# Two-layer trunk on one core: all adaLN sums on TensorE, in four column groups of 32, by half chunks

## The chip, the cores and the metric

The kernel runs as one program on one of the eight NeuronCores of a Trainium2 chip. The metric is device time in microseconds (us) of one execution; lower is better. The engines are TensorE (PE in the profile; its weight loads are the row PEld), VectorE (DVE), ScalarE (ACT), GpSimd (POOL) and the DMA queue that SyncE issues (SP, in the profile SPq). All five run their own instruction streams in order and wait for each other by semaphores.

## What is computed

Two groups of tokens, 512 latent and 128 context, go through two layers with the same weights. Each layer is an adaLN-modulated RMSNorm, an input projection, four mixers (three attentions and an mLSTM), a gated merge with an output projection, then a second modulated RMSNorm and a SwiGLU feed-forward. The change concerns one small part of it, the adaLN vectors:

```python
def _adaln(cvec, w, b):
    m = jnp.dot(jax.nn.silu(cvec), w) + b
    return jnp.split(m, 6, axis=-1)

def _modulate(xn, shift, scale):
    return xn * (1 + scale) + shift
...
    sh1, sc1, gt1, sh2, sc2, gt2 = _adaln(c_ctx, w_mod[l], b_mod[l])
    h = _modulate(_rmsnorm(xp, norm1_g[l]), sh1, sc1)
    ...
    xp = xp + gt1 * _merge(...)
    xp = xp + gt2 * _swiglu(_modulate(_rmsnorm(xp, norm2_g[l]), sh2, sc2), w_ffn_in[l], w_ffn_out[l])
```

Per layer, two vectors of 1024 (one of each token group, called v = 0 and v = 1) are multiplied with a 1024 x 6144 matrix `w_mod[l]`. The 6144 columns are shift, scale and gate of the first norm (w = 0) and of the second (w = 1), each 1024 wide. Everything is float32, and the matrix of one layer is 25 MB.

## The kernel before, in words

**The main stream.** Weights come from HBM as 128 x 1024 blocks (`wload`, L399). ScalarE makes a rounded float32r copy `hi` (L404), VectorE the rest `lo` (L405), and TensorE forms each product with three float32r matmuls, hi by hi, hi by lo and lo by hi (`mm3`, L416 to L418). There are two raw buffers and five of each of hi and lo. From the fifth feed-forward column block on, the feed-forward runs a seven-product scheme in `ff_pair` (matmuls on L1825 to L1827), in which VectorE combines PSUM results between the products (L1839, L1843, L1846) before a PSUM bank may be used again; the weight splits of that part are on L453 and L454. PSUM has eight banks: three of `acc`, two each of `S` and `T`, one of `O`.

**The adaLN columns** are cut into chunks of 512, twelve to a layer. A chunk has eight k-tiles of 128 rows.

- *Chunks 0 to 3 of layer 0* (shift and scale of the very first norm) are made in `start()`. For the first four k-tiles of a chunk (two in the last chunk) VectorE multiplies the tile by the silu column of v and adds it to an accumulator 128 x 512 (L490, L492). The other k-tiles go to TensorE as plain float32 matmuls with two columns of weights (L608). Two matmuls with `sel` add the rows of the accumulators into the same PSUM bank (L610). Then the two rows are copied (L611), turned into columns with four transposes (L614) and stored in `modr` (L615). After the second and the fourth chunk, `mod_cols` (L645 to L647) and the modulation (L625, L628, L629) make half of `hT`, the input of the first projection.
- *The other 20 chunks* are the background, a generator `adaln_all` that is advanced by the main stream. A load brings one k-tile of 256 KB (L512, four buffers `wm`). VectorE sums v = 0 into `msum0` (L490, L492), ScalarE multiplies for v = 1 (L485) and GpSimd adds (L488). At the end of a chunk, eight 128 x 128 transposes put the sums on the free axis (L501), and VectorE reduces them to columns (L502). Gates go on through a bias (L528), a transpose (L532) and DRAM.

**What sets the order.** The kernel is recorded in one order, and a scheduler places each engine's instructions by priority. `tick()` (L390) is called at each step of the main stream and adds `bg[0]` to a credit; each whole credit advances the background by one step. The rate is 0.14 in the mixers, 0.8 in the last four merges of a layer (M20 to M23), 0.1 in the `ff_pair` part and 0.3 in the feed-forward's output products. `bg_until` runs the generator until the chunks that a norm or a gate needs are there.

```python
BG_MIX, BG_FREE, BG_PAIR, BG_OUT = 0.14, 0.8, 0.1, 0.3
...
    def tick():
        bg[1] += bg[0]
        bg_steps(int(bg[1]))
        bg[1] -= int(bg[1])
```

Of the kernel before, what the change touches and what calls it, by code (L numbers as in the profile page):

```python
# [17 lines left out]
P = 128  # L18
# [69 lines left out]

BG_MIX, BG_FREE, BG_PAIR, BG_OUT = 0.14, 0.8, 0.1, 0.3
# [137 lines left out]
def trunk(ctx: ExitStack, tc: tile.TileContext, a: dict, depth: int):  # L227
# [130 lines left out]
    V.memset(sel, 0.0)  # L358
    V.memset(sel[:, 0:4:3], 1.0)
# [14 lines left out]
    with tc.high_priority(offset=8 * WPRI):  # L374
        SY.dma_start(csil.rearrange("p k v -> p (k v)"), a["cc"])
        S.activation(csil, csil, AF.Silu)
    hT = cp.tile([P, KT, 2, NTOK], F32R, name="hT")
# [91 lines left out]


    bg_after = {}

    def newest():
        return list(nc.cur_bb.bb.instructions)[-1]

    def behind(eng):
        if eng in bg_after:
            after(newest(), bg_after.pop(eng), "the norm and what follows it go before the background")

    def adaln_acc(accs, w, kk, tmp=None):  # L480

        for v in range(2):
            s = csil[:, kk, v:v + 1]
            if v and tmp is not None:
                S.activation(accs[v][:, :512] if kk == 0 else tmp, w, AF.Copy, scale=s)  # L485
                behind("S")
                if kk:
                    G.tensor_tensor(accs[v][:, :512], accs[v][:, :512], tmp, ALU.add)  # L488
            elif kk == 0:
                V.tensor_scalar(accs[v][:, :512], w, s, None, ALU.mult)  # L490
            else:
                V.scalar_tensor_tensor(accs[v][:, :512], w, s, accs[v][:, :512], ALU.mult, ALU.add)  # L492
            if v == 0 and tmp is not None:
                behind("V")

    def adaln_cols(dst, accs):

        for v in range(2):
            ps = (bT if v else bS)()
            for j in range(4):  # L500
                T.transpose(ps[:, j * P:(j + 1) * P], accs[v][:, P * j:P * j + P], ident)  # L501
            V.tensor_reduce(dst(v), ps.rearrange("p (j n) -> p j n", j=4), AX.X, ALU.add)  # L502

    have = set()

    def adaln_all(items):


        def load(x):
            if x < KT * len(items):  # L510
                (l, ch), k = items[x // KT], x % KT
                SY.dma_start(wm_tiles[x % 4], a["w_mod"][l, P * k:P * k + P, 512 * ch:512 * ch + 512])  # L512
                behind("load")

        load(0)
        load(1)
        for i, (l, ch) in enumerate(items):
# [6 lines left out]
            if (ch // 2) % 3 == 2:  # L524
                adaln_cols(lambda v: gcol[:, 4 * v:4 * v + 4], msum)
                w, h = ch // 6, ch % 2
                for v in range(2):
                    V.tensor_tensor(gcol[:, 4 * v:4 * v + 4], gcol[:, 4 * v:4 * v + 4], bgate[:, l, w, 4 * h:4 * h + 4],  # L528
                                    ALU.add)
# [19 lines left out]
    def start():  # L549
# [49 lines left out]
        for x, ch in enumerate(order):  # L599
# [9 lines left out]
            for v in range(2):  # L609
                T.matmul(ps[:2], sel[:, 2 * v:2 * v + 2], accs[v][:, :512], start=False, stop=(v == 1))  # L610
# [1456 lines left out]
```

## Time and profile before

| | |
|---|---|
| median of 3 runs | 2729.99 us (2727.19 to 2732.35) |
| the profiled execution | 2728.15 us |
| its span (first to last instruction) | 2726.4 us |
| PE busy | 2665.0 us, 98% |
| DVE, ACT, POOL busy | 78%, 53%, 27% |
| mean granted TensorE clock | 0.996 of full speed |
| HBM read | 252.73 MB |

How to read it: a matmul's busy time includes its way through the array, which overlaps the next one, so a row's mean duration (some 310 ns) is more than the step from one matmul to the next (0.11 us at 256 columns). What a matmul costs is read from the step between starts. The idle time of PE is the span minus its busy time. The chain of work is followed back from the last instruction, at each step to what released it.

### The profile page before, as it was taken

The page shows a single profiled execution, that of the slowest core. Times are in us where ns is not written, and L with a number is a line of the kernel's source. Part 1 is how long each engine was busy: PE and PEld are TensorE (multiplying, and loading weights), DVE is VectorE, ACT ScalarE, POOL GpSimd, SP SyncE. Part 2 cuts the span into 40 slices and gives each one's busy share as a digit, 9 for nine tenths or more (in the row PEclk, how much of TensorE's full clock was granted, in tenths as well). Part 3 has the DMA queues.
Part 4 walks back from the last instruction along what each step waited for, and adds up shares of the span by engine and source line. Part 5 has one row for each costly group of instructions (what it writes and reads, how often), then busy time and mean ns, then how long its engine had stood idle before and what let it go on. Part 6 is the DMA issues. An engine that isn't in the chain of part 4 may idle for free.

```text
span 2726.4 us, 51965 instructions
## 1 busy us (share of the span) xinstructions
PE 2665.0 (98%) x19514; PEld 2618.7 (96%) x19514; DVE 2125.9 (78%) x4780; ACT 1434.3 (53%) x3298; POOL 732.1 (27%) x650
## 2 busy tenths in 40 slices
PE   8999999999999999999999999999999999999998
PEld 5999999999999999999999999999999999999998
DVE  8776668889978778888777866778888767586957
ACT  6864446666644543444468743556666545333433
POOL 2000112112035326454330101112002342243433
PEclk9999999999999999999999999999999999999999
DMA  7323322112135333333232332212112342222222
GB/s 279 103 88 101 110 66 87 49 52 91 47 122 188 99 109 102 112 101 109 93 104 92 119 92 88 92 62 71 58 56 78 126 160 75 83 85 78 86 90 74
DMA packets 123580, 264.29 MB, mean 97 GB/s; under 512 B 14192, under 2 KB 40144, under 8 KB 123328
## 3 DMA queue, kind: packets, MB, share of 16 engines
q1 hardware_dynamic: 123328, 260.97, 29.7%
q8 instruction: 153, 2.51, 0.4%
q14 instruction: 99, 0.81, 0.1%
HBM read 252.73 MB, written 7.95 MB: 96 GB/s over the span
## 4 chain that ended last, share of the span: by engine, by line
PE 81%; DVE 10%; ACT 3%; issue 3%; DMA 2%; POOL 1%; DVEq 0%; SPq 0%; POOLq 0%; ACTq 0%
PE acc L416 18%; PE acc L417 18%; PE acc L418 18%; PE acc L1825 3%; PE acc L1826 3%; PE acc L1827 3%; PE O L1243 2%; PE T L1233 2%; DVE msum L492 1%; PE O L1826 1%; PE O L1825 1%; PE O L1827 1%; DVE wlo L405 1%; DMA wm<-w_mod 1%; PE S L1200 1%
## 5 line engine op out<-in xcount | busy, mean ns | idle before, releaser
L416 PE MATMUL acc<-hT,whi 128*128 128x256 f32 (+1 forms) x2240 | 698.0, 313 | 11.6 <-DVE hT L688 5.6
L417 PE MATMUL acc<-hT,whi 128*128 128x256 f32 (+1 forms) x2240 | 696.7, 311 | 2.3 <-DVE hT L629 1.3
L418 PE MATMUL acc<-hT,wlo 128*128 128x256 f32 (+1 forms) x2240 | 693.1, 310 | 0.0
L404 ACT CAST whi<-raw 128x512 fp32r<-128x512 f32 (+1 forms) x488 | 298.9, 620 | 371.8 <-PE acc L417 172.6
L405 DVE TENSOR_TENSOR wlo<-raw,whi 128x512 fp32r<-128x512 f32 (+1 forms) x488 | 373.2, 768 | 130.6 <-ACT whi L404 124.4
L416 PEld LDWEIGHTS acc<-hT,whi 128*128 128x128 f32 x2240 | 420.5, 188 | 17.0 <-DVE hT L688 6.5
L417 PEld LDWEIGHTS acc<-hT,whi 128*128 128x128 f32 x2240 | 422.3, 189 | 5.7 <-DVE hT L629 2.1
L418 PEld LDWEIGHTS acc<-hT,wlo 128*128 128x128 f32 x2240 | 421.9, 188 | 0.8
L488 POOL TENSOR_TENSOR msum<-msum,mtmp 128x512 f32<-128x512 f32 x140 | 206.7, 1476 | 227.4 <-ACT msum L485 133.1
L1623 POOL TENSOR_TENSOR m<-m,f 128x256 f32<-128x256 f32 x96 | 98.8, 1031 | 485.1 <-DVE f L1621 319.3
L1651 POOL TENSOR_TENSOR big<-big,t 128x256 f32<-128x256 f32 x150 | 127.9, 862 | 241.1 <-DVE t L1650 234.8
L748 ACT CAST pth<-T 128x512 fp32r<-128x512 f32 (+1 forms) x232 | 117.9, 520 | 112.2 <-PE T L1233 53.9
L485 ACT ACTIVATE mtmp<-wm,csil 128x512 f32<-128x512 f32 x140 | 101.4, 724 | 127.6 <-POOL msum L488 114.9
L749 DVE TENSOR_TENSOR ptl<-T,pth 128x512 fp32r<-128x512 f32 (+1 forms) x232 | 137.4, 603 | 34.3 <-ACT pth L748 33.8
L416 PE MATMUL acc<-big,whi 128*128 128x256 f32 (+1 forms) x512 | 159.6, 312 | 4.0 <-ACT f L1615 4.0
L453 ACT CAST whi<-of 128x512 fp32r<-128x512 f32 x144 | 88.7, 620 | 141.5 <-PE acc L418 49.8
L416 PE MATMUL acc<-whi,m 128*128 128x256 f32 x560 | 157.6, 283 | 5.0 <-DVE t L1650 5.0
L1650 DVE TENSOR_TENSOR t<-acc,P 128x256 f32<-128x256 f32 x200 | 82.9, 420 | 102.1 <-PE acc L418 75.1
L418 PE MATMUL acc<-big,wlo 128*128 128x256 f32 (+1 forms) x512 | 160.8, 314 | 0.0
L417 PE MATMUL acc<-big,whi 128*128 128x256 f32 (+1 forms) x512 | 159.2, 311 | 0.0
L417 PE MATMUL acc<-wlo,m 128*128 128x256 f32 x560 | 156.7, 281 | 0.0
L418 PE MATMUL acc<-whi,m 128*128 128x256 f32 x560 | 156.5, 280 | 0.0
(464 smaller groups left out, 7905.1 us busy)
## 6 DMA issues: line engine op xcount, KB each, us to landing
raw<-wflat SPq DMA_DIRECT2D x236, 512.0 KB
wm<-w_mod SPq DMA_DIRECT2D x160, 256.0 KB
raw<-wflat SPq DMA_DIRECT2D x120, 256.0 KB
q<-wflat SPq DMA_DIRECT2D x48, 256.0 KB
kv<-nbias SPq DMA_DIRECT2D x16, 576.0 KB
kv<-mdr SPq DMA_DIRECT2D x16, 320.0 KB
big<-x_sample SPq DMA_DIRECT2D x8, 512.0 KB
P<-gt_d SPq DMA_DIRECT2D x32, 128.0 KB
```

What stands on the lines that cost most here:

```text
L404: S.copy(hi[:, :n], raw[:, s0:s0 + n])
L405: V.tensor_tensor(lo[:, :n], raw[:, s0:s0 + n], hi[:, :n].bitcast(F32), ALU.subtract)
L416: T.matmul(ps, lhs(k, 0), rhs(k, 0), start=(k == 0), stop=False)
L417: T.matmul(ps, lhs(k, 0), rhs(k, 1), start=False, stop=False)
L418: T.matmul(ps, lhs(k, 1), rhs(k, 0), start=False, stop=(k == kn - 1))
L488: G.tensor_tensor(accs[v][:, :512], accs[v][:, :512], tmp, ALU.add)
L748: S.copy(hi[:, :n], ps[:, :n])
L749: V.tensor_tensor(lo[:, :n], ps[:, :n], hi[:, :n].bitcast(F32), ALU.subtract)
L1651: (V if n == 3 else G).tensor_tensor(xs[tt][:, 256 * n:256 * n + 256], xs[tt][:, 256 * n:256 * n + 256], t[:, :256], ALU.add)
L1825: T.matmul(ps, f(0), ops[name](k, 0), start=first and k == 0, stop=False, **more)
L1826: T.matmul(ps, f(0), ops[name](k, 1), start=False, stop=False, **more)
L1827: T.matmul(ps, f(1), ops[name](k, 0), start=False, stop=k == 3, **more)
```

## The change

All adaLN sums are matmuls. The two silu columns of a k-tile are padded with zeros to a weight block of 32 columns, `cw[:, k, :]`. The eight k-tiles of a sum are dealt to four column groups of the array: k-tile k writes PSUM partitions 32 (k % 4) to 32 (k % 4) + 31, so each group adds two k-tiles up. A second small matmul ("turn") takes the copied sums as weights (128 x 128) and `sel` as the moving operand of two columns: `sel` has ones at 32 g + v, so it adds the four groups and turns rows to columns at once. `adaln_sums` and `adaln_turn` are used by the first norm with 512 columns, where VectorE copies the sums, and by the background with 256 columns (half a chunk), where ScalarE copies them.

The background has three buffers of 512 KB (four k-tiles of 256 columns) in place of four of 256 KB, two loads to a half chunk; a load waits for the four matmuls that read its buffer. Its rate is 0.15 in the mixers and stays so through M20 to M23; the other rates are gone, and it is not advanced in the feed-forward. In the recorded order, 13 of the 20 chunks are done by the end of layer 0's output projection and the last by the second merge of layer 1's mLSTM branch (M31); before, four of the chunks were made in layer 0's feed-forward and about four in each layer's M20 to M23.

```diff
-BG_MIX, BG_FREE, BG_PAIR, BG_OUT = 0.14, 0.8, 0.1, 0.3
+BG_MIX = 0.15
...
-    wm_tiles = [cp.tile([P, 512], F32, name=f"wm{i}") for i in range(4)]
-    msum = [cp.tile([P, 512], F32, name=f"msum{v}") for v in range(2)]
-    mtmp = cp.tile([P, 512], F32, name="mtmp")
+    wm_tiles = [cp.tile([P, 1024], F32, name=f"wm{i}") for i in range(3)]
+    msum = cp.tile([P, 256], F32, name="msum")
+    cw = cp.tile([P, 8, 32], F32, name="cw")
...
+    def adaln_sums(ps, w, n):
+        for k in range(KT):
+            g = 32 * (k % 4)
+            T.matmul(ps[g:g + 32, :n], cw[:, k, :], w(k), start=(k < 4), stop=(k >= 4))
+
+    def adaln_turn(pc, sums, n):
+        for j in range(n):
+            T.matmul(pc[:, 2 * j:2 * j + 2], sums[:, P * j:P * j + P], sel[:, 0:2], start=True, stop=True)
...
-            for k in range(KT):
-                adaln_acc(msum, wm_tiles[(KT * i + k) % 4], k, mtmp)
-                load(KT * i + k + 2)
-                yield True
...
+        for i, (l, ch, hf) in enumerate(halves):
+            ps = bS()
+            adaln_sums(ps, lambda k: wm_tiles[(2 * i + k // 4) % 3][:, 256 * (k % 4):256 * (k % 4) + 256], 256)
+            S.copy(msum, ps[:, :256])
+            load(2 * i + 3)
+            load(2 * i + 4)
+            yield True
+            pc = bT()
+            adaln_turn(pc, msum, 2)
...
         for x, ch in enumerate(order):
-            accs = [ofs.take() for _ in range(2)]
+            sums = ofs.take()
             ps = acc()
...
+            adaln_sums(ps, lambda k: bufs[4 * x + k // 2][k % 2], 512)
+            V.tensor_copy(sums[:, :512], ps)
             pc = acc()
+            adaln_turn(pc, sums, 4)
...
-            if name == "M20":
-                bg[0] = BG_FREE
...
-                    bg[0] = BG_PAIR
...
-                bg[0] = BG_OUT
```

Three places show what moves; rows are in program order, and no time is in them.

TensorE in the first norm, second and third chunk (ch 2 and ch 1): before, four k-tiles of each went to TensorE, then the two sums of VectorE's accumulators (`of`).

```order
L608 MATMUL acc_164<-kv_3_211,csil 2x512 x2
L614 MATMUL acc_163<-ident,of_1_356 128x2 x4
L608 MATMUL acc_164<-kv_4_212,csil 2x512 x2
L610 MATMUL acc_164<-of_3_378,sel 2x512
L610 MATMUL acc_164<-of_4_379,sel 2x512
L614 MATMUL acc_162<-ident,of_3_378 128x2 x4
L608 MATMUL acc_163<-q_1_215,csil 2x512 x2
L608 MATMUL acc_163<-q_2_216,csil 2x512 x2
```

Now all eight k-tiles are there, 32 rows high, and a turn of four (L485) ends each chunk.

```order
L480 MATMUL acc_162<-kv_1_208,cw 32x512
L480 MATMUL acc_162<-kv_2_209,cw 32x512 x2
L480 MATMUL acc_162<-kv_3_210,cw 32x512 x2
L480 MATMUL acc_162<-kv_4_211,cw 32x512 x2
L485 MATMUL acc_160<-sel,of_2_370 128x2 x4
L480 MATMUL acc_161<-kv_5_212,cw 32x512 x2
L480 MATMUL acc_161<-kv_6_213,cw 32x512 x2
L480 MATMUL acc_161<-q_1_214,cw 32x512 x2
L480 MATMUL acc_161<-q_2_215,cw 32x512 x2
L485 MATMUL acc_162<-sel,of_3_407 128x2 x4
```

The chunk's matmuls on TensorE go from six to eight, with no accumulator of VectorE to wait for.

TensorE in the mixers of layer 0: the transposes that ended a background chunk before stand between the matmuls of a projection.

```order
L418 MATMUL acc_164<-whi_140,hT 128x256
L501 MATMUL S_166<-ident,msum_69 128x128 x4
L416 MATMUL acc_164<-whi_141,hT 128x256
L417 MATMUL acc_164<-wlo_146,hT 128x256
L418 MATMUL acc_164<-whi_141,hT 128x256
```

Now half a chunk's eight narrow matmuls stand there together (in other places in two or more pieces), and the turn of two follows.

```order
L419 MATMUL acc_160<-hT,whi_140 128x384
L480 MATMUL S_164<-wm_67,cw 32x256 x4
L480 MATMUL S_164<-wm_65,cw 32x256 x4
L420 MATMUL acc_160<-hT,whi_140 128x384
L421 MATMUL acc_160<-hT,wlo_145 128x384
L419 MATMUL acc_160<-hT,whi_140 128x384
L420 MATMUL acc_160<-hT,whi_140 128x384
L485 MATMUL T_166<-sel,msum 128x2
L1463 MATMUL S_163<-kv_24_2375,P_155 128x129
L485 MATMUL T_166<-sel,msum 128x2
```

The 320 narrow matmuls of the background stand in 66 such unbroken runs: 22 of eight, 13 of four, 8 of five or seven and 23 of one to three.

VectorE in layer 0's feed-forward, at one `ff_pair`: before, the sums of the background (L492) stand between the combinations L1839, L1843 and L1846 that free the PSUM banks.

```order
L454 TENSOR_TENSOR wlo_147<-of_32_10072,whi_142 128x512
L492 SCALAR_TENSOR_TENSOR msum_69<-wm_67,csil,msum_69 128x512
L1839 TENSOR_TENSOR f_153<-acc_163,f_153 128x320
L454 TENSOR_TENSOR wlo_143<-q_24_10068,whi_138 128x512
L492 SCALAR_TENSOR_TENSOR msum_69<-wm_68,csil,msum_69 128x512
L1843 TENSOR_TENSOR f_153<-acc_164,f_153 128x320
L492 SCALAR_TENSOR_TENSOR msum_69<-wm_65,csil,msum_69 128x512
L1846 TENSOR_TENSOR f_152<-O_169,f_153 128x320
```

Now only the weight splits (L457) stand between the same combinations (L1817, L1821, L1824).

```order
L457 TENSOR_TENSOR wlo_145<-of_28_10065,whi_140 128x512
L1817 TENSOR_TENSOR f_151<-acc_161,f_151 128x320
L457 TENSOR_TENSOR wlo_141<-q_24_10061,whi_136 128x512
L1821 TENSOR_TENSOR f_151<-acc_162,f_151 128x320
L457 TENSOR_TENSOR wlo_142<-raw_134,whi_137 128x512
L1824 TENSOR_TENSOR f_150<-O_167,f_151 128x320
```

Three sums of the background have left this piece of VectorE's queue.

## Rows read from the trace of the kernel before

**Rows 1.** The page, busy time, share of the span and instructions by engine:
```profile
PE 2665.0 (98%) x19514; PEld 2618.7 (96%) x19514; DVE 2125.9 (78%) x4780; ACT 1434.3 (53%) x3298; POOL 732.1 (27%) x650
```

**Rows 2.** The page, chain that ended last, shares by engine:
```profile
PE 81%; DVE 10%; ACT 3%; issue 3%; DMA 2%; POOL 1%; DVEq 0%; SPq 0%; POOLq 0%; ACTq 0%
```

**Rows 3.** Stretches: us; busy PE, PEld, DVE, ACT, POOL; PE clock, DMA share, GB/s:
```profile
0.00:38.00 38.00, 29.14 (x100) 11.34 (x101) 29.23 (x76) 20.27 (x54) 4.77 (x12) 1.00 0.98 361
409.00:424.00 15.00, 12.91 (x82) 12.65 (x81) 14.81 (x27) 9.90 (x20) 6.40 (x5) 0.89 0.35 110
860.00:930.00 70.00, 68.28 (x556) 67.19 (x555) 51.86 (x95) 34.21 (x80) 37.08 (x35) 1.00 0.43 147
930.00:1290.00 360.00, 347.35 (x2537) 344.00 (x2537) 302.10 (x455) 154.31 (x297) 168.40 (x129) 0.99 0.33 106
1189.00:1198.00 9.00, 5.14 (x21) 4.89 (x20) 9.00 (x12) 3.44 (x7) 4.45 (x3) 0.63 0.43 128
2181.00:2290.00 109.00, 107.35 (x832) 106.56 (x830) 74.43 (x133) 51.58 (x114) 46.20 (x44) 1.00 0.35 121
2290.00:2720.00 430.00, 424.68 (x3168) 423.21 (x3168) 316.97 (x522) 163.95 (x330) 155.89 (x137) 1.00 0.26 84
```

**Rows 4.** Timeline of VectorE in layer 0's feed-forward (start, us, engine, line, operation):
```profile
1189.30 0.48 DVE L1839 TENSOR_TENSOR f<-acc,f 128x320 f32<-128x320 f32 x1
1189.70 1.35 DVE L454 TENSOR_TENSOR wlo<-q,whi 128x512 fp32r<-128x512 f32 x1
1190.98 1.75 DVE L492 SCALAR_TENSOR_TENSOR msum<-wm,csil,msum 128x512 f32<-128x512 f32 x1
1192.65 0.48 DVE L1843 TENSOR_TENSOR f<-acc,f 128x320 f32<-128x320 f32 x1
```

**Rows 5.** Timeline of PE at the same place (idle before, releaser in brackets):
```profile
1193.18 0.64 PE L1825 MATMUL acc<-hT,whi 128*128 128x320 f32 x1 [3.86 <-DVE f L1843]
```

**Rows 6.** Groups by line and shape: count, busy us, mean ns, idle before:
```profile
L492 DVE SCALAR_TENSOR_TENSOR msum<-wm,csil,msum 128x512 f32<-128x512 f32 x140 | 136.7, 976 | 5.0 <-DMA wm<-w_mod 3.6 <-DVE wlo L405 0.3
L501 PE MATMUL T<-ident,msum 128*128 128x128 f32 x80 | 13.4, 274 | 0.0
L501 PE MATMUL S<-ident,msum 128*128 128x128 f32 x80 | 12.5, 272 | 0.0
L610 PE MATMUL acc<-of,sel 128*2 128x512 f32 x16 | 7.5, 592 | 0.0
```

**Rows 7.** Chain that ended last, pieces (start, us, engine, output, line, count):
```profile
27.78 3.52 PE acc L608 x8
42.59 0.18 DVE modr L615
443.24 1.01 PE acc L1162 x10
694.59 0.87 PE T L1233 x8
872.62 8.38 DMA wm<-w_mod
```

**Rows 8.** Timeline of PE in the first norm, narrow and full-width matmuls in turn:
```profile
35.00 2.74 PE L608 MATMUL acc<-big,csil 128*2 128x512 f32 x6
37.67 0.38 PE L416 MATMUL acc<-hT,whi 128*128 128x256 f32 x1
37.98 1.02 PE L608 MATMUL acc<-big,csil 128*2 128x512 f32 x2
```

**Rows 9.** Timeline of PE in layer 0's mixers, around a gate's transpose (8 columns):
```profile
283.14 0.27 PE L532 MATMUL T<-ident,gcol 128*8 128x128 f32 x1
283.17 0.36 PE L418 MATMUL acc<-whi,hT 128*128 128x256 f32 x1
283.37 0.28 PE L416 MATMUL acc<-whi,hT 128*128 128x256 f32 x1
283.49 0.28 PE L417 MATMUL acc<-wlo,hT 128*128 128x256 f32 x1
```

More of the change, by code (lines that the diff above doesn't have):

```diff
@@ L376, in trunk @@
         S.activation(csil, csil, AF.Silu)
+    with tc.high_priority(offset=8 * WPRI):
+        V.memset(cw, 0.0)
+        V.tensor_copy(cw[:, :, 0:2], csil)
     hT = cp.tile([P, KT, 2, NTOK], F32R, name="hT")
@@ L468, in mod_slice @@
         return modr[:, w, s, 4 * (ch % 2):4 * (ch % 2) + 4, :]
[L471 to L502, printed above, removed]
-    have = set()
+    have = set()
+    modulated = [None]
+    def adaln_sums(ps, w, n):
+        for k in range(KT):
+            g = 32 * (k % 4)
+            T.matmul(ps[g:g + 32, :n], cw[:, k, :], w(k), start=(k < 4), stop=(k >= 4))
@@ L506, in adaln_all @@
+    def adaln_turn(pc, sums, n):
+        for j in range(n):
+            T.matmul(pc[:, 2 * j:2 * j + 2], sums[:, P * j:P * j + P], sel[:, 0:2], start=True, stop=True)
     def adaln_all(items):
+        halves = [(l, ch, hf) for l, ch in items for hf in range(2)]
         def load(x):
[L510 to L513, printed above, removed]
@@ L515, in adaln_all @@
-        load(0)
-        load(1)
-        for i, (l, ch) in enumerate(items):
-            for k in range(KT):
-                adaln_acc(msum, wm_tiles[(KT * i + k) % 4], k, mtmp)
-                load(KT * i + k + 2)
-                yield True
-            yield True
-            yield True
[L524 to L529, printed above, removed]
-                yield True
+            if x < 2 * len(halves):
+                (l, ch, hf), q = halves[x // 2], x % 2
+                c0 = 512 * ch + 256 * hf
+                SY.dma_start(wm_tiles[x % 3].rearrange("p (k n) -> p k n", k=4),
+                             a["w_mod"][l, 512 * q:512 * q + 512, c0:c0 + 256].rearrange("(k p) n -> p k n", p=P))
@@ new lines, in adaln_all @@
+        for x in range(3):
+            load(x)
+            after(list(nc.cur_bb.bb.instructions)[-1], modulated[0], "the first norm goes before the background")
+        for i, (l, ch, hf) in enumerate(halves):
[7 more added lines that the diff above has]
+            adaln_turn(pc, msum, 2)
+            view = pc[:, 0:4].rearrange("p (j v) -> p j v", j=2)
+            if (ch // 2) % 3 != 2:
+                V.tensor_copy(mod_slice(ch)[:, 2 * hf:2 * hf + 2, :], view)
+                if hf:
+                    have.add((l, ch))
+                yield True
+                continue
+            w, h = ch // 6, ch % 2
+            for v in range(2):
+                V.tensor_tensor(gcol[:, 4 * v + 2 * hf:4 * v + 2 * hf + 2], view[:, :, v],
+                                bgate[:, l, w, 4 * h + 2 * hf:4 * h + 2 * hf + 2], ALU.add)
+            yield True
+            if hf:
```

29 lines of the change are left out of this document (5 added, 24 removed).

## The prediction, made before the changed kernel ran

> **What bounds the kernel now.** I read the page first. PE is busy for 2665.0 of 2726.4 us, so it is idle for 61.4 us [rows 1], and 81% of the chain that ended last is PE, 10% DVE [rows 2]. A busy PE need not be at its peak, but the steps between its matmuls are steady: 0.12 us at 256 columns [rows 9]. So TensorE is the bound nearly everywhere. Work taken off VectorE, ScalarE and GpSimd can return at most the idle time of PE and what a low clock adds behind it; work put on TensorE is paid in full unless it runs inside the array beside other work. That is the balance to be drawn.
>
> The stretches then say where PE is idle [rows 3]. The first 38 us hold 8.9 us. Layer 0's feed-forward (930 to 1290 us), through which the background runs, holds 12.65 us in 360; layer 1's (2290 to 2720 us), with no background, 5.32 in 430. The two stages M20 to M23, with the fast background, hold 1.72 and 1.65 us. The largest single wait shows how it comes: two combinations of one `ff_pair`, L1839 and L1843, stand 3.35 us apart on VectorE because a weight split and an accumulation L492 of 1.75 us lie between them [rows 4]; PE waits 3.86 us for L1843 [rows 5]. The stretch from 1189 to 1198 us then has a granted clock of 0.63, which is some 6.7 of 9 us at the lower of the two levels, 1.2 GHz; PE had been idle just before [rows 3].
>
> **The change, part by part.** The sum is made against the profiled execution, 2728.15 us; the median of the runs, 2729.99, is 1.8 us above it, so the two agree within 0.1%.
>
> *Removed from PE:* 160 transposes L501 [rows 6]. Eight transposes of this shape take 0.87 us on the chain [rows 7], 0.109 each: -17.4 us.
>
> *Added, the turns:* 40 half chunks with two matmuls. A float32 matmul that is no transpose leaves two records: the code has eight calls of L610, the trace 16 records [rows 6]. So 160 records of two columns, with 128 columns of weights. L1162 is of that form, ten in 1.01 us [rows 7]: +16.2 us. Turns and transposes cancel.
>
> *Added, the sums:* 320 calls, 640 records of 256 columns. Eight records of 512 columns take 3.52 us [rows 7], and six are 2.74 us long with a duration of 0.592 for the last, so they start 0.43 us apart [rows 6, 8]; half the columns make 0.215. One after the other this is 640 x 0.215 = 137.6 us. No row shows matmuls in different column groups, since all narrow ones of before stand at the first columns, so I bound it from both sides. No overlap gives 137.6. If everything ran four abreast, 34.4. In between lies what the order of the records makes likely: the two records of a call go to the same group, one behind the other; if the engine starts its matmuls in order, the second record of a call can overlap only the first of the next call, which is in another group. Then each call costs one record, and an unbroken run costs one more: (320 + 66) x 0.215 = 83.0 us. I take this, because it needs groups that work at once but no matmul that overtakes another. The one overlap in the trace is of little help: a gate's transpose (8 columns) and the full-width matmul behind it start 0.03 us apart, but the next start is 0.20 us later; the 0.23 us together are what the two cost in a row [rows 9].
>
> *Added, going in and out of the narrow form:* six narrow records from 35.00 end their stream at 35.00 + 6 x 0.43 = 37.58; one full-width matmul follows, and the next narrow one starts at 37.98 [rows 8]. That is 0.40 us for a matmul that costs 0.12, so one way out and one in cost 0.28. The background makes 66 such visits: +18.5 us. The bounds are zero (if a longer queue hides it) and twice that.
>
> A page of the Trainium skill, TensorEngine Tiling (Array Packing), section Tiling Modes, says that a change of the tiling mode, unlike a change of the tile, drains TensorE. The 0.28 us of [rows 8] agree.
>
> *Saved in layer 0's feed-forward:* its idle time falls to layer 1's share, 5.32 x 360/430 = 4.5 of 12.65 us: -8.2. The low clock after the long wait goes too; 6.7 us at half speed gave away 3.3: -3.3.
>
> *Saved elsewhere:* the stretch from 409 to 424 us has 2.09 us of idle PE and 1.65 us lost at a clock of 0.89 [rows 3], with accumulations in VectorE's queue: -3.7. Of the 3.4 us in the two M20 to M23 stages I take 1 off. The rest of the mixers' idle time occurs alike in layer 1, and I leave it. Together with the feed-forward: -16.2 us.
>
> *The first norm:* the DMA engines are 98% busy over 38 us at 361 GB/s [rows 3], so the loads end near there, while the fourth chunk's columns are stored at 42.59 [rows 7]. With pairs, PE needs 4 x 9 x 0.43 = 15.5 us for all sums and follows the loads; copy, turn and store add some 1.5 us: -3. One after the other, 64 records of 0.43 and 32 turn records make 30.7 us in place of 52 records, 22.4 us: +8, less some 3 for waits on VectorE's accumulators and their copies, so +5.
>
> *At nothing:* 40 copies of 128 x 256 on ScalarE, which is 47% idle [rows 1]; the loads, which move the same bytes with one half chunk's lead; VectorE's small copies. If that cover fails, PE itself stands at the head of its queue and waits, with the whole projection behind it; that is a rival below.
>
> Sum: 2728.15 - 17.4 + 16.2 + 83.0 + 18.5 - 16.2 - 3 = **2809 us**, 3% slower than before.
>
> **The rivals.**
>
> *No overlap at all* (chance 0.23). The records of the trace before show every narrow float32 matmul 0.43 us behind the last, and [rows 9] shows no time gained. 2728.15 - 17.4 + 16.2 + 137.6 + 18.5 - 16.2 + 5 = 2872 us.
>
> *Four groups abreast* (0.15). Four calls abreast then take the time of one call, two records or 0.43 us: 30 runs of five to eight calls at 0.86 and 36 of up to four at 0.43 make 41.3 us. 2728.15 - 17.4 + 16.2 + 41.3 + 18.5 - 16.2 - 3 = 2768 us. For it: nothing in the first record of a group depends on another group. Against: the pairs of records.
>
> The Trainium skill, TensorE: Matmul & The Clock Gate, Part 3, says that matmuls in different column groups run at once, gives 2.38 times for three of them, and also says that matmuls start and end in program order. The factor alone would make the sums 137.6/2.38 = 58 us, an estimate, and the whole 2784; the order speaks for pairs. No run here shows either yet.
>
> *Relief outweighs the sums* (0.14): faster. VectorE is what PE waits for in most places, and the 136.7 us of L492 [rows 6] leave its queue, with ScalarE's and GpSimd's shares. Full overlap (34.4 us), visits that cost nothing, and all 61.4 us of idle time gone but the first 38 us' 8.9 would give 2728.15 - 1.2 + 34.4 - 52.5 = 2709 us. It decides where the relief exceeds what the sums cost, here 33 us; I count 19. Layer 1's feed-forward, without background, still has its 5.3 us, so full relief is not to be had.
>
> *PE before a late load* (0.04). Until now VectorE and ScalarE took the waits for `wm`; the longest on the chain is 8.38 us [rows 7]. If ten of the 40 half chunks met half of that, some 40 us come on top of the forecast: 2849.
>
> **How the numbers follow.** The forecast of pairs has 0.44. About 0.2% is what a measurement of this kernel can tell from no change, 5.5 us. Faster: most of the relief case, 0.10; the same: 0.04 from it; slower: all the rest, 0.86. The range of 8 in 10 leaves out the relief case and the worst of the serial one (whose visits cost twice as much): 2750 to 2880 us. The likeliest case's own range is 2790 to 2840: visits from nothing to twice 18.5, and sums up to a quarter of the way from pairs to no overlap, 14 us more.
>
> **What would show each step.** The starts of eight narrow matmuls: 0.43 us to a call of 256 columns means no overlap, 0.215 means pairs, 0.11 four abreast. A full-width matmul right before or behind them starts 0.1 to 0.2 us late. L501 is gone, and the turns cost 0.10 us a record. PE's idle time in layer 0's feed-forward is near 4.5 us in 360, with no low clock; the mixers of both layers grow by all of the sums. The first norm's last columns are stored near 39.5 us. I am wrong if the mixers do not grow by more than the feed-forward shrinks, or if PE's idle time grows in front of the narrow matmuls.

## The result, and the profile of the changed kernel

| | before | changed |
|---|---|---|
| median of 4 runs, us | 2729.58 (2727.19 to 2732.35) | 2755.09 (2753.98 to 2755.62) |
| ratio, 95% interval | | 1.0086 (1.0074 to 1.0097) |
| profiled execution and its span, us | 2728.15, 2726.4 | 2755.43, 2753.7 |

The changed kernel is 0.9% slower: 25.5 us by the medians, 27.3 by the profiled executions, where the forecast was 81 us more than the profiled execution before. Of the kernel without background, below, one execution of four ran slow (3222.64 us at a granted clock of 0.75) and is left out of its median. The direction held and the time lies in the range, but two thirds of the expected loss is not there. So the question is what the forecast priced too high, and where time came back.

The page of the changed kernel, with the lines that answer to [rows 1, 2]:

```profile
PE 2711.4 (98%) x20182; PEld 2636.0 (96%) x20182; DVE 1894.9 (69%) x4593; ACT 1346.4 (49%) x3178; POOL 517.2 (19%) x510
...
PE 88%; DVE 4%; ACT 4%; issue 2%; DMA 2%; POOL 1%; SPq 0%; DVEq 0%; POOLq 0%; ACTq 0%
```

PE is idle for 42.3 us of the span (2753.7 - 2711.4), 19 less than before, and VectorE's share of the chain fell from 10% to 4%. VectorE lost 231 us of work, GpSimd 215.

The groups of the new lines, by shape (count, busy us, mean ns of one, idle before):

```profile
L480 PE MATMUL S<-wm,cw 128*32 128x256 f32 x640 | 54.7, 387 | 0.0
L485 PE MATMUL T<-sel,msum 128*128 128x2 f32 x160 | 20.5, 231 | 0.0
```

The counts are the forecast's, 640 and 160, but 640 records of 0.215 us cannot lie in 54.7 us of busy time unless several run at once. The timeline of PE in the mixers shows how many (start, us, engine, line, operation):

```profile
75.46 0.60 PE L949 MATMUL T<-ident,P 128*128 128x128 f32 x4
75.99 1.07 PE L480 MATMUL S<-wm,cw 128*32 128x256 f32 x16
76.99 0.44 PE L931 MATMUL S<-m,q 128*128 128x384 f32 x1
77.27 0.34 PE L932 MATMUL S<-m,q 128*128 128x384 f32 x1
77.44 0.28 PE L419 MATMUL acc<-hT,whi 128*128 128x256 f32 x1
```

Sixteen records, the eight calls of a half chunk, take 1.07 us from the first start to the last end, and the next matmul starts 1.00 us behind the first. Pairs would take 1.9 us, one after the other 3.4. A visit's price follows from the same rows: 1.00 us, plus 0.09 in front (the last of four transposes starts 3 x 0.109 behind 75.46, at 75.79, and the first narrow record 0.20 later in place of 0.11), plus 0.11 behind (0.28 to the next start where the same shape then takes 0.17). That is 1.20 us for eight calls. Worked out so for every visit, five to eight calls cost 1.20 us at the median, one to four calls 0.76; so four calls cost 0.43 and going in and out 0.34. All 66 visits cost 64.9 us, where the forecast had 83.0 + 18.5; 1.7 of the 64.9 are a wait for VectorE that lies right behind one visit.

The stretches of the changed kernel that answer to [rows 3] (us; busy PE, PEld, DVE, ACT, POOL; PE clock, DMA share, GB/s). Places lie later by what the kernel had lost up to there:

```profile
0.00:38.00 38.00, 24.58 (x124) 12.36 (x125) 16.21 (x54) 20.49 (x54) 5.07 (x13) 0.94 0.97 355
33.00:40.00 7.00, 7.00 (x28) 3.98 (x27) 2.89 (x8) 0.45 (x2) 0.00 (x0) 0.51 0.91 305
422.00:437.00 15.00, 15.00 (x111) 14.11 (x110) 13.81 (x38) 9.46 (x27) 0.11 (x1) 1.00 0.34 112
890.00:960.00 70.00, 70.00 (x579) 68.64 (x577) 34.74 (x79) 26.23 (x66) 19.53 (x23) 1.00 0.33 114
962.00:1322.00 360.00, 357.36 (x2645) 355.91 (x2644) 262.82 (x427) 135.51 (x265) 126.17 (x109) 1.00 0.27 86
2208.00:2317.00 109.00, 107.94 (x831) 107.56 (x829) 55.35 (x111) 44.12 (x103) 29.23 (x32) 1.00 0.30 100
2320.00:2750.00 430.00, 422.57 (x3154) 421.10 (x3152) 315.52 (x519) 164.02 (x331) 154.59 (x138) 1.00 0.26 84
```

Layer 0's feed-forward has 2.64 us of idle PE in 360 (12.65 before), the place around 422 us none (2.09), the two M20 to M23 stages 0 and 1.06 (1.72 and 1.65). The first norm got worse: 13.4 us of idle PE in 38 (8.9 before), and from 33 to 40 us a granted clock of 0.51, which is the lower level, 1.2 GHz, nearly throughout. PE had stood almost idle just before, as the timelines of VectorE and of PE show (idle before a row, and its releaser, in brackets):

```profile
29.14 0.90 DVE L610 CAST hT<-f 128x640 fp32r<-128x640 f32 x2 [1.95 <-ACT f L607]
29.95 1.56 DVE L611 TENSOR_TENSOR hT<-f,hT 128x640 fp32r<-128x640 f32 x2
31.42 0.49 DVE L610 CAST hT<-f 128x640 fp32r<-128x640 f32 x1
31.82 0.68 DVE L594 COPY of<-acc 128x512 f32<-128x512 f32 x1
...
43.16 0.17 DVE L597 COPY modr<-acc 128x8 f32<-128x8 f32 x1 [1.15 <-PE acc L485]
```

```profile
26.80 2.10 PE L480 MATMUL acc<-q,cw 128*32 128x512 f32 x8
32.56 1.41 PE L485 MATMUL acc<-sel,of 128*128 128x2 f32 x8 [3.67 <-DVE of L594]
```

The third chunk's sums end at 28.9 us, but their copy L594 stands on VectorE behind the modulation of the first half (L610, L611), which itself waits for ScalarE. The turn starts at 32.56, and what follows it runs at the lower clock. The last columns are stored at 43.16 us, against 42.59 before [rows 7] and 39.5 in the forecast.

### The profile page after: what moved, and what is told of

It is laid out like the page before. It is cut to its first block, busy times and chain, and to the rows that moved or that the text cites. A ratio compares the mean times of both kernels' runs of the same rounds, so it can differ in the third digit from the quotient of the medians.

```text
span 2753.7 us, 52642 instructions
## 1 busy us (share of the span) xinstructions
PE 2711.4 (98%) x20182; PEld 2636.0 (96%) x20182; DVE 1894.9 (69%) x4593; ACT 1346.4 (49%) x3178; POOL 517.2 (19%) x510
## 4 chain that ended last, share of the span: by engine, by line
PE 88%; DVE 4%; ACT 4%; issue 2%; DMA 2%; POOL 1%; SPq 0%; DVEq 0%; POOLq 0%; ACTq 0%
PE acc L419 20%; PE acc L420 20%; PE acc L421 19%; PE acc L1803 3%; PE acc L1804 3%; PE acc L1805 3%; PE O L1223 2%; PE T L1213 2%; PE S L480 2%; PE O L1804 1%; PE O L1803 1%; PE O L1805 1%; DMA raw<-wflat 1%; PE S L1180 1%; PE S L1181 1%
## 5 line engine op out<-in xcount | busy, mean ns | idle before, releaser
L408 DVE TENSOR_TENSOR wlo<-raw,whi 128x512 fp32r<-128x512 f32 (+1 forms) x488 | 343.7, 707 | 218.8 <-ACT whi L407 213.3
L1631 POOL TENSOR_TENSOR big<-big,t 128x256 f32<-128x256 f32 x150 | 120.2, 808 | 305.4 <-DVE t L1630 299.3
L456 ACT CAST whi<-of 128x512 fp32r<-128x512 f32 x144 | 88.9, 620 | 146.9 <-PE acc L421 51.1
L1803 PE MATMUL acc<-hT,whi 128*128 128x320 f32 x432 | 133.3, 309 | 1.5 <-DVE f L1821 1.5
L1805 PE MATMUL acc<-hT,wlo 128*128 128x320 f32 x432 | 133.0, 308 | 0.0
```

The costliest lines, as they stand in the source:

```text
L408: V.tensor_tensor(lo[:, :n], raw[:, s0:s0 + n], hi[:, :n].bitcast(F32), ALU.subtract)
L1631: (V if n == 3 else G).tensor_tensor(xs[tt][:, 256 * n:256 * n + 256], xs[tt][:, 256 * n:256 * n + 256], t[:, :256], ALU.add)
L1803: T.matmul(ps, f(0), ops[name](k, 0), start=first and k == 0, stop=False, **more)
L1805: T.matmul(ps, f(1), ops[name](k, 0), start=False, stop=k == 3, **more)
```

## The experiments

Sixteen kernels ran. Their times are compared with the changed kernel's median, 2755.09 us; a ratio is to the kernel before, run beside them. Where a place is said to be longer or shorter, the times from the same plain matmul to the same plain matmul in two profiles are compared.

### One column group, and two

G stands for the number of groups; `msum` is zeroed once, so that the turn can still add four groups.

```
+        V.memset(msum, 0.0)
...
-            adaln_sums(ps, ...)
-            S.copy(msum, ps[:, :256])
+            for k in range(KT):
+                g = 32 * (k % G)
+                T.matmul(ps[g:g + 32, :256], ..., start=(k < G), stop=(k >= KT - G))
+            S.copy(msum[:32 * G], ps[:32 * G, :256])
```

With G = 1:

> The changed kernel with all eight background calls of a half chunk in one column group instead of four (the other rows of the sum are zeroed once). Work on the other engines is the same. Theory 'four abreast' (the four groups' matmuls run at once, so 320 calls cost 0.107 us each, and each visit another 0.34 us): without other groups the calls cost 0.43 each, 137.6 us, and some 69 visits 23.5, in all 161 against 64.9 in the changed kernel, so 96 us more: about 2851 us. Rival 'paid as pairs' (the starts 7 ns apart in the trace are not what is paid; the calls cost 83 us as forecast, and the stalls that went are larger than counted): 137.6 - 83.0, 55 us more: about 2810 us.

One run: 2846.8 us, 92 more than the changed kernel. Timeline of PE:

```profile
78.05 0.60 PE L956 MATMUL T<-ident,P 128*128 128x128 f32 x4
78.58 3.64 PE L487 MATMUL S<-wm,cw 128*32 128x256 f32 x16
82.14 0.44 PE L938 MATMUL S<-m,q 128*128 128x384 f32 x1
```

With G = 2:

> The same with two column groups. 'Four abreast' (as many at once as there are groups): 68.8 us of calls and 68 visits at 0.34, 92 us against 64.9, so 27 us more: about 2782 us, with narrow starts two by two, 0.215 us apart. 'Paid as pairs': two groups are enough for what is already paid, no change: 2755 us within 3.

One run: 2783.8 us, 29 more. The same place:

```profile
75.46 0.60 PE L956 MATMUL T<-ident,P 128*128 128x128 f32 x4
75.99 1.92 PE L487 MATMUL S<-wm,cw 128*32 128x256 f32 x16
77.84 0.44 PE L938 MATMUL S<-m,q 128*128 128x384 f32 x1
```

The same sixteen records take 3.64, 1.92 and 1.07 us in one, two and four groups. All visits together cost 159.7, 98.7 and 64.9 us; a visit of eight calls 3.77, 2.05 and 1.20. Less 0.34 for going in and out, that is 0.43 us for each call, each two and each four. The rival "paid as pairs" is out: with it two groups would have cost nothing more. The whole runs agree with the visits within 5 us: 94.8 and 33.7 us were added there.

### Two calls of one group in a row

```
-            adaln_sums(ps, ..., 256)
+            adaln_sums(ps, ..., 256,
+                       order=(0, 4, 1, 5, 2, 6, 3, 7))
```

> The changed kernel with the background's calls in the order of contraction blocks 0, 4, 1, 5, 2, 6, 3, 7: two calls of one group, four records, stand one behind the other in the program before the next group's. Theory 'overtaking' (a record of another group starts although records of an earlier group wait in front of it): as long as the engine sees far enough, still four abreast, a visit of eight calls 1.20 us and the time 2755 within 4; if it sees only the next one or two records, runs fall back towards one or two at once. Rival 'program order' (a record starts only when all before it have started): a run of eight calls has 16 records of 0.215 us, of which only the last of one group and the first of the next lie together, 13 x 0.215 = 2.8 us against 0.86; over 320 calls some 60 to 78 us more: 2815 to 2833 us.

One run: 2766.8 us, 11 more. It lies between the two, nearer to overtaking. Timeline of PE, a full visit and one of two calls:

```profile
75.22 1.09 PE L480 MATMUL S<-wm,cw 128*32 128x256 f32 x16
...
305.28 1.05 PE L480 MATMUL S<-wm,cw 128*32 128x256 f32 x4
```

Sixteen records still take 1.09 us, though four records of one group now stand in front of the next group's first. If they started in the program's order, it would be 2.8. So records of other groups do overtake those that wait for their own group. What the order costs is elsewhere: a visit of two calls now holds one group only, four records one after the other in 1.05 us, and visits of three and four calls hold a whole group too. Visits of two to four calls cost 1.15 to 1.28 us, where they cost 0.70 to 0.86. All visits cost 77.3 us, 12.4 more, and that is the whole loss.

### All eight calls in one visit

```
+            with tc.high_priority(offset=WPRI):
                 adaln_sums(ps, ..., order=(4, 1, 6, 3, 0, 5, 2, 7))
```

> The changed kernel with the background's calls in the order 4, 1, 6, 3, 0, 5, 2, 7 and ahead of the other work in the scheduler's order, so that all eight calls of a half chunk stand together once both loads are in: 40 visits of eight instead of 66 of one to eight. Theory 'a visit has its own price' (0.34 us whatever its calls, and a visit of one to three calls pays a whole row of four): 40 x 1.20 = 48 us against 64.9, 17 us less: about 2738 us, at least 26 x 0.34 = 9 us less (2746). Rival 'calls alone are paid' (the 0.34 us is what the calls themselves take to run out, and neighbours hide it), or the sums now hold up TensorE for a load: no change or slower, 2755 us or above.

2744.18 us, ratio to the kernel before 1.0041 (1.0027 to 1.0055): 11 us less than the changed kernel. The group of the narrow matmuls (count, busy us, mean ns of one, idle before), for which the changed kernel had 54.7:

```profile
L480 PE MATMUL S<-wm,cw 128*32 128x256 f32 x640 | 42.8, 385 | 0.0
```

The 40 visits cost 49.4 us in place of 64.9, as expected to within 1.4 us. The visit has a price of its own, and short visits waste the array.

### The first norm alone, and the background alone

The first: the kernel before with the change's sums and turns in `start()`, and nothing else.

```
-            accs = [ofs.take() for _ in range(2)]
-            ...
+            sums = ofs.take()
+            adaln_sums(ps, lambda k: bufs[4 * x + k // 2][k % 2], 512)
+            V.tensor_copy(sums[:, :512], ps)
+            adaln_turn(pc, sums, 4)
```

> The kernel before with the change's first norm alone (sums and turns of its four chunks on TensorE in four column groups); the background stays on VectorE, ScalarE and GpSimd. Theory 'no gain there' (in the changed kernel TensorE stood 34.9 us beyond its work up to the first norm's end against 35.7 before, since the copy of the third chunk's sums stands on VectorE behind the modulation of the first half): within 2 us of the kernel before. Rival 'the forecast's step' (VectorE's share of the sums ended the wait, so 3 us go): 3 us less than the kernel before.

2731.94 us, ratio 1.0005 (0.9995 to 1.0014): no gain there. A gain of 3 us, the forecast's step, lies outside the interval.

The second: the changed kernel with the sums of `start()` as before.

```
+    sel4 = cp.tile([P, 4], F32, name="sel4")
...
-            adaln_sums(ps, lambda k: bufs[4 * x + k // 2][k % 2], 512)
+            ...
+                adaln_acc(accs, w, k)
+            ...
```

> The changed kernel with the first norm of the kernel before (its sums on VectorE and TensorE, its transposes). If the first norm gives nothing, this is the changed kernel's time, 2755 us within 3, and its difference to the kernel before is the whole of the change. If the forecast's step of 3 us is there, it is 2758 us. If the change's first norm lost time to the lower clock between 33 and 40 us, it is 2752 us or less.

2775.95 us, ratio 1.0161 (1.0148 to 1.0174), 21 us above the changed kernel. None of the three numbers. The excess grows through the whole kernel, even in layer 1's feed-forward, where nothing of the change runs. There its row of 100 us (columns as in the stretches above) holds 750 matmuls:

```profile
2500.00:2600.00 100.00, 99.72 (x750) 99.51 (x749) 72.72 (x110) 35.36 (x67) 39.45 (x35) 1.00 0.26 80
```

and that of the changed kernel, at the same work, 754:

```profile
2480.00:2580.00 100.00, 99.72 (x754) 99.51 (x753) 73.48 (x112) 36.42 (x69) 39.85 (x35) 1.00 0.25 81
```

Plain 320-column matmuls start 147.2 ns apart on average in place of 145.7. Of this kernel only the 16-byte table `sel4` reaches so far: tiles that are made after it are laid 32 bytes further.

### Where the tiles lie

The same kernel with `sel4 = gcol[:, 0:4]`, a tile that is free at that time:

> The run with the background alone on TensorE took 2776 us, 21 more than the changed kernel, and its profile shows the plain 320-column matmuls of the last layer's feed-forward, where nothing of the change runs, 147.2 ns apart instead of 145.7. It had one more table of 16 bytes a partition among the first tiles, which moves all later tiles by so much. Here the same kernel with this table laid over a tile that is free then, so that nothing is moved. Theory 'place': the matmuls are 145.7 ns apart again and the time is the changed kernel's, 2755 us, or with the first norm's difference 2750 to 2758. Rival 'first norm': what differs is the old first norm itself, the time stays at 2776 within 3.

2754.68 us, ratio 1.0084 (1.0068 to 1.0100): the changed kernel's time, and 145.7 ns again. So the background is the whole of the change, and the place was the 21 us. In the kernel before the step is 145.8 ns, so no difference of place shows between it and the changed kernel.

Two runs meant to move tiles by an unused tile moved none: it was laid into room that another tile had left, and in the program all other tiles lie where they lay.

```
+    pad = cp.tile([P, 4], F32, name="pad")
+    V.memset(pad, 0.0)
```

> The changed kernel with an unused tile of 16 bytes a partition among the first tiles, as the run with the background alone had it. Theory 'place': all later tiles lie 16 bytes further, the 320-column matmuls are 147.2 ns apart instead of 145.7, and the time is some 19 us longer, 2770 to 2778 us. Rival: the place does nothing, 2755 us within 2.

2756.38 us, ratio 1.0092 (1.0077 to 1.0107). With `[P, 16]` in the kernel before:

> The kernel before with an unused tile of 64 bytes a partition at the same spot. If only a shift that is no multiple of 64 bytes costs, the time is the kernel before's within 3 us; if every other place than the present one costs, it is some 19 us longer; if there are better ones, it may be shorter. Theory 'place by 64': no change.

2731.78 us, ratio 0.9997 (0.9986 to 1.0007). Both only repeat the kernels they were made from and say nothing of the place. The next one moves a tile for certain, with room in front of it and behind:

```
-    hT = cp.tile([P, KT, 2, NTOK], F32R, name="hT")
+    hT = cp.tile([P, 16 + 2 * KT * NTOK], F32R, name="hT")[:, 8:8 + 2 * KT * NTOK]...
```

> The changed kernel with the normalized activations, which all projections read, placed 32 bytes further in each partition; the tiles behind it move by 64, those ahead not at all. In the run with the background alone they and all tiles behind them lay 32 bytes further, and the 320-column matmuls were 147.2 ns apart instead of 145.7; with the table over a free tile they were 145.7 again. Theory 'place': 147 ns again for the matmuls that read these activations, and 10 to 21 us more than the changed kernel, 2765 to 2776 us. Rival 'not the place' (something else of that kernel, such as its order): 2755 us within 2.

2769.66 us, ratio 1.0133 (1.0117 to 1.0148), 15 us more, and in the row of 100 us 750 matmuls again:

```profile
2500.00:2600.00 100.00, 99.71 (x750) 99.51 (x749) 72.29 (x112) 36.37 (x69) 36.88 (x33) 1.00 0.27 85
```

The matmuls that read `hT` start 147.2 ns apart in layer 1's feed-forward, in place of 145.5; those that read `kv`, now 64 bytes further, 146.4 in place of 146.0. In the run with the background alone, where `kv` lay 32 bytes further, these took 146.9. So moving `hT` by 32 bytes and the tiles behind it by 64 makes most of the 21 us, and the shift of those other tiles by 32 goes with the rest.

### The first norm's copy ahead

```
+            with tc.high_priority(offset=2 * WPRI):
                 V.tensor_copy(sums[:, :512], ps)
                 ...
```

> The changed kernel with the copies, turns and stores of the first norm's sums ahead of all else in the scheduler's order. Theory 'the copy waits behind the modulation' (28.7 us sums done, copy at 31.8, TensorE idle until 33.6 and at 1.2 GHz from 33.1 to 39.9): the wait of 4.3 us shrinks to about 1.5 us and the low clock starts later or not at all: 3 to 8 us less, 2747 to 2752 us. Rival 'the loads end the first norm' (what follows waits for the modulation of the second half, which waits for its last loads): no change, 2755 us within 2.

2756.58 us, ratio 1.0091 (1.0077 to 1.0106): no change, but the edit did not do what it was to do. VectorE's timeline has the copy in its old place:

```profile
31.69 0.48 DVE L611 CAST hT<-f 128x640 fp32r<-128x640 f32 x1
32.09 0.68 DVE L595 COPY of<-acc 128x512 f32<-128x512 f32 x1
```

The priority did not change the order on VectorE, so whether an earlier copy would gain stays open.

### No background at all

```
     def adaln_all(items):
-        halves = ...
-        ...
+        V.memset(grow, 0.5)
+        ...
+        have.update(items)
+        yield True
```

> The changed kernel without any background: the modulation tables and gates are constants, only the first norm's four chunks are computed. It measures what either kernel pays for its background. Theory 'direct price and relief' (the changed kernel pays its visits, 64.9 us, and turns, 15.1, and almost nothing else; the kernel before paid 17.4 for transposes and 35 in waits made by its background's work on VectorE, ScalarE and GpSimd): 2670 to 2680 us. Rival 'disturbed all the same' (the change's background still makes waits in the mixers, and the kernel before's made fewer than 35): 2660 us or less would put more waits to both; 2690 or more would mean that part of the 80 us lies beside other waits.

2676.13 us, ratio 0.9795 (0.9772 to 0.9817), as the first theory has it. From its page:

```profile
PE 2632.7 (98%) x19374; PEld 2600.8 (97%) x19374; DVE 1885.1 (70%) x4531; ACT 1330.4 (50%) x3138; POOL 519.9 (19%) x510
```

This gives the bill of both kernels, by the profiled spans. The kernel before pays 2726.4 - 2677.1 = 49.3 us for its background: 17.4 for its transposes and 31.9 in waits. Of these 17.0 show as idle PE (61.4 us against 44.4); the rest lies in starts that come late while the matmul before still counts as busy, for the usual step at 256 columns is 117 ns in both profiles, and the mean granted clock 0.996 against 0.995. The changed kernel pays 76.6: 64.9 for visits and 15.1 for turns make 80.0, so 3.4 of them lie beside waits that PE has anyway. The difference in waits, 35.3 us, is what the change gave back. The profiled executions are single ones: by the medians of that round, 2732.19 and 2676.13, the kernel before pays 56 us, so these figures hold within some 7 us.

By place, against the kernel without background (the places given in the time of the kernel before): it is 14.4 us longer up to 840 us (the first norm and layer 0's mixers), 5.1 from there to 909 us, 18.3 to 1321 us (the second norm and layer 0's feed-forward), and 11.5 in layer 1. The changed kernel is 46.4, 4.8, 1.9 and 23.5 us longer.

### The background kept out of the feed-forward, on the old engines

```
-BG_MIX, BG_FREE, BG_PAIR, BG_OUT = 0.14, 0.8, 0.1, 0.3
+BG_MIX, BG_FREE, BG_PAIR, BG_OUT = 0.31, 0.8, 0.0, 0.0
```

> The kernel before, whose background stays on VectorE, ScalarE and GpSimd, with other rates: 0.31 of a step per matmul group in the mixers instead of 0.14, and none in the feed-forward, so that the second half of layer 0's chunks is summed before the feed-forward instead of in it. Theory 'the feed-forward was disturbed' (the 15 us that layer 0's feed-forward lost in the change come from its having no background beside it, and any way of keeping it out gives them): 12 to 15 us less there, and up to 8 us more of waits in the mixers, whose VectorE takes twice the steps: 2715 to 2726 us. Rival 'relief of VectorE' (the gain needs the sums off VectorE; moved into the mixers they make as many waits there): 2730 us or more, with the mixers 12 us or more longer.

2743.99 us, ratio 1.0047 (1.0034 to 1.0060): slower. Layer 0's feed-forward gives back 13.0 us, as the first theory has it, though five sums of VectorE's still run in it (34 before), but layer 0's mixers lose 19 and layer 1 loses 13. The rival has the total right.

### Four chunks on TensorE, sixteen as before

Only the four chunks that the kernel before sums beside layer 0's feed-forward go to TensorE, by half chunks in four groups; the rate of the output products falls to 0.03, and that of the mixers is 0.15.

```
+    def narrow(l, ch):
+        return l == 1 and ch < 4
...
+                    with tc.high_priority(offset=WPRI):
+                        for k in (6, 1, 4, 3, 2, 5, 0, 7):
+                            g = 32 * (k % 4)
+                            T.matmul(ps[g:g + 32, :256], cw[:, k, :], ...)
```

> The kernel before with four of its twenty background chunks, those of the next layer's first norm that it sums beside layer 0's feed-forward, on TensorE in four column groups by half chunks (eight visits, together once the loads are in); the other sixteen stay on VectorE, ScalarE and GpSimd in the mixers, and no vector step of the background is left in the feed-forward. The kernel before is 23 us longer there than the kernel without background. Theory 'the feed-forward pays most': 8 visits x 1.20 and 16 turns x 0.19 make 12.6 us in place of 23: 10 us less than the kernel before, about 2720 us. Rival 'relief is spread' (what the change gave back came from VectorE's lighter load in the mixers): no gain, 2728 us or more.

2740.98 us, ratio 1.0030 (1.0018 to 1.0041): a miss. The feed-forward won, but the mixers ahead of it lost 10 us, where the rate of 0.15 was the main difference. Two runs took this apart. The same with 0.14, and with the background halted in the feed-forward once the four chunks are done:

> The run of four narrow chunks with the mixers' rate of the kernel before (0.14) and no vector step of the background in the feed-forward. Theory 'the feed-forward pays for its vector work': the mixers up to the second norm as in the kernel before, and 10 us less in the feed-forward: about 2721 us; 2727 or less bears it out. Rival 'relief is spread': what the eight visits and sixteen turns cost (12.6 us) is about what the feed-forward wins, so 2729 to 2735 us.

2726.90 us, ratio 0.9983 (0.9974 to 0.9992). It beats both kernels, the one before by 4.5 us, just outside its interval and just under what I called distinguishable. The stretch of the second norm and layer 0's feed-forward, between the same plain matmuls, before:

```profile
909.00:1321.00 412.00, 399.35 (x2960) 396.00 (x2959) 339.60 (x529) 179.78 (x359) 193.19 (x153) 0.99 0.32 101
```

and in this run:

```profile
912.00:1315.00 403.00, 398.84 (x3020) 393.17 (x3019) 300.70 (x498) 165.04 (x337) 151.48 (x130) 1.00 0.32 99
```

PE's idle time falls from 12.65 to 4.16 us. One chunk of eight vector steps still runs in the feed-forward, from 1263 to 1274 us, so the expectation that none is left did not come true. The 10 us of the first theory were 8 there, and 3 were lost ahead of the stretch, where three of the visits now lie.

And the rate alone, in the kernel before:

```
-BG_MIX, BG_FREE, BG_PAIR, BG_OUT = 0.14, 0.8, 0.1, 0.3
+BG_MIX, BG_FREE, BG_PAIR, BG_OUT = 0.15, 0.8, 0.1, 0.3
```

> The kernel before with 0.15 background steps per matmul group in the mixers instead of 0.14, and nothing else. If the 10 us that the mixers lost in the run of four narrow chunks came from this rate (the steps fall at other places beside the same work, and other waits form), this run is 5 to 12 us longer than the kernel before; if they came from the narrow chunks' loads or tables, it is within 3 us of it.

2757.59 us, ratio 1.0094 (1.0080 to 1.0108): 26 us, more than the expected 5 to 12, and as much as the whole change costs. The work is the same; the steps fall beside other matmuls. The costliest group's row has 10 us of it as waits (count, busy, mean ns, idle before):

```profile
L416 PE MATMUL acc<-hT,whi 128*128 128x384 f32 (+1 forms) x2240 | 701.7, 315 | 21.9 <-DVE hT L688 4.7 <-DVE t L1134 4.6 <-DVE m L1621 3.5
```

The same group in the kernel before, on its page:

```profile
L416 PE MATMUL acc<-hT,whi 128*128 128x256 f32 (+1 forms) x2240 | 698.0, 313 | 11.6 <-DVE hT L688 5.6
```

and in the changed kernel, whose background also runs at 0.15:

```profile
L419 PE MATMUL acc<-hT,whi 128*128 128x256 f32 (+1 forms) x2240 | 698.3, 313 | 7.5 <-DVE hT L668 4.6
```

The mean granted clock is 0.993 in place of 0.996, which over 2755 us is some 8 us. So the 31.9 us of waits in the kernel before are no fixed price of vector work; they are what is left at a rate that suits it. At 0.15 they are, with the lower clock, 26 us more. Nor has a rate a price of its own: of the profile's 28.6 us 20 came in layer 1, where the run of four narrow chunks with the same 0.15 lost 6. The change raised this rate as well, for steps of another size; other rates of the changed kernel were not run.

## Why the prediction was wrong in size

The forecast was 2809 us, the profiled execution took 2755.4; 53.6 us are to be explained.

- **The bound** was read rightly. What was put on TensorE is paid: the changed kernel's 80.0 us of visits and turns show in the time but for 3.4.
- **Transposes and turns:** the 160 transposes are gone (-17.4), and the turns cost 15.1 us, counted from start to start (0.094 a record), against 16.2. 1.1 us.
- **The sums: here the forecast failed.** The step was: "if the engine starts its matmuls in order, the second record of a call can overlap only the first of the next call, which is in another group. Then each call costs one record". The engine does not start them in order across groups. Four calls of four groups take 0.43 us together, so the runs cost 42.5 us (64.9 less 66 x 0.34) in place of 83.0. That is the rival of four abreast (41.3), which had 0.15. I gave the order in the program the weight that only a trace of two groups could have had.
- **Going in and out:** 0.34 us a visit against 0.28, 22.4 us against 18.5. The mechanism held. Sums and visits together are 36.6 us of the 53.6. That all five engines run their instructions in order, as said ahead, does not hold for TensorE's narrow records.
- **Layer 0's feed-forward:** -8.2 and -3.3 were foreseen. Its stretch is 16.4 us shorter, set against the kernel without background (18.3 to 1.9); 32 transposes of it were 3.5 us, so some 13 us of waits and low clock went. Right, and a little short.
- **409 to 424 us, M20 to M23:** the 3.7 us went, and of the 1.72 and 1.65 us of idle PE 2.3, against 1.
- **The rest of the mixers: the second step that failed.** "The rest of the mixers' idle time occurs alike in layer 1, and I leave it." Layer 1 had background in its mixers too, so being alike in both layers was no sign that it had another cause. The run without background shows 31.9 us of waits that it made in the kernel before; with the 3.4 us of the changed kernel's own work that lie beside other waits, 35.3 came back, where the forecast had 16.2 + 3. That is the other 16.1 us; with the first norm's 3 missing and some 2.6 more from the feed-forward and M20 to M23, the rest of the mixers gave about 16.5, where the forecast had nothing.
- **The first norm:** -3 was wrong. The sums follow the loads, but the third chunk's copy and turn wait behind the modulation of the first half, PE stands idle for 3.67 us, and the lower clock follows; the last columns come at 43.16 us. That an earlier copy would have gained the 3 us is not shown.
- **The relief rival** (faster) named the right mechanism and too large a gain: it decided where the relief exceeds the cost of the sums, 33 us with full overlap and free visits. The relief was 35.3 us, but the visits were not free.

The two pages that the prediction drew on: TensorEngine Tiling (Array Packing), section Tiling Modes, of the Trainium skill says that a change of the mode drains the engine; the 0.34 us of each visit agree. TensorE: Matmul & The Clock Gate, Part 3, of the Trainium skill says that matmuls in different column groups run at once, and the trace agrees, with a factor of 4 for four groups (3.77 - 0.34 against 1.20 - 0.34 us for eight calls). It also says that matmuls start and end in program order. The run with two calls of a group in a row does not bear that out across groups, 1.09 us against 2.8, and the measurement decides.

## What to carry to other kernels

Narrow float32 matmuls in four column groups ran four at once here, also with two calls of a group in a row, so price a run by its longest group and add a third of a microsecond for each visit; put the calls together, since a visit of one call costs as much as one of four. When work leaves an engine that others wait for, measure its bill by taking the work out altogether, because waits that look the same in every layer can belong to it. And before a small loss or gain is put down to an idea, move the rate or the order a little: here one hundredth in a rate was worth as much as the whole change, and far more than the 4.5 us by which four narrow chunks beat the kernel before.

## What the runs showed of the hardware that I had not expected

- Records of other column groups overtake those that wait for their own: sixteen records in 1.07 us in four groups, 1.92 in two, 3.64 in one, and 1.09 with four records of each group in a row.
- Where a tile lies matters: with the activations 32 bytes further in each partition, the 320-column matmuls that read them start 147.2 ns apart in place of 145.5, and the kernel takes 15 us more. Why 32 bytes cost that was not found.
- The lower clock level appeared in the first norm of the changed kernel (0.51 granted from 33 to 40 us), after PE had stood idle for all but 0.2 of the 3.8 us from 28.7 to 32.5:

```profile
28.70:32.50 3.80, 0.19 (x1) 0.00 (x0) 3.36 (x7) 3.52 (x9) 1.37 (x2) 1.00 1.04 378
```
